# First projections by halves of the features, and rotary scores over 128 rows, in a two-layer hybrid decoder trunk

## The chip, the cores and the metric

The kernel runs on one core of a Trainium2 chip. The metric is the time of one execution on the device in microseconds (us), lower is better. TensorE is called PE in the profile, VectorE DVE, ScalarE ACT, GpSimd POOL and SyncE SP; PEld is TensorE's weight load, which goes beside its matmuls.

## The reference

Two layers on 512 tokens of 1024 features, f32. Each layer is a half-step SwiGLU, a mixer of three branches, and a second half-step SwiGLU, each with a LayerNorm behind it.

```python
def swiglu(x, w_gate, w_up, w_down):               # 1024 -> 2816 -> 1024
    return (jax.nn.silu(x @ w_gate) * (x @ w_up)) @ w_down
...
def causal_block_attention(q_nope, q_rope, k_nope, k_rope, v):   # 4 heads, 128 + 64 features
    ...
        s = (jnp.einsum('bqhd,bkhd->bhqk', q_nope[:, q0:q1], k_nope[:, :q1])
             + jnp.einsum('bqhr,bkr->bhqk', q_rope[:, q0:q1], k_rope[:, :q1])).astype(jnp.float32) * scale
...
    for l in range(DEPTH):
        h = layer_norm(DEEPNORM_ALPHA * h + 0.5 * swiglu(h, ...), ln1_g[l], ln1_b[l])
        mix = hybrid_mixer(h, cos, sin, ...)
        h = layer_norm(DEEPNORM_ALPHA * h + mix, ln2_g[l], ln2_b[l])
        h = layer_norm(DEEPNORM_ALPHA * h + 0.5 * swiglu(h, ...), ln3_g[l], ln3_b[l])
```

The mixer projects x by one combined matrix. Its branches are a gated DeltaNet (short convolutions of 4 taps on q, k and v, a delta rule in chunks of 64, an output norm), a convolution of 31 taps over 512 channels, and a latent attention with 4 heads, whose score has a part of 128 features per head and a rotary part of 64, for which all heads share one key. Three sigmoid gates weight them.

## The kernel before

**Numbers.** Each f32 product with a weight is taken as three matmuls of a rounded f32 form (`mm3`): ACT casts the high part, DVE subtracts it to get the low part, for x (`xh`, `xl`) and for every weight (`s` tiles from a `raw` buffer). The scores and the delta rule's small products go in plain f32, each of which the trace shows as two instructions.

**Order.** All instructions are recorded by a planner class and issued afterwards, so nearly every row of the profile names one line, L287. The planner keeps a cost for each instruction (`_cost`), a priority (the clock of PE at which it was recorded, plus a bias that `pl.stream` sets), and the number of free buffers, and lists instructions for each engine by simulating them. A changed cost or bias can therefore move instructions anywhere in the program. Engines run their lists in order. All DMAs are issued from SP.

**Start.** x comes in 8 pieces `s<-in_x` of 128 tokens by 512 features. `to_features` transposes each on PE with an identity (`ident`), casts it to `xh` on ACT, subtracts on DVE to `xl`, and copies the f32 form to `xf` on ACT. Each FFN begins with `proj_first`: four banks (gate and up for the first two blocks of 128 hidden columns), each by half of the tokens (256 columns) over all 8 feature blocks of 128. The first weights are loaded as whole blocks of 512 KB. After these, pairs of blocks go through `seven`, a Strassen-like scheme of seven products, for which `block_sums` prepares differences of x blocks on DVE (8 subtractions and 16 halves of splits per FFN).

**Mixer.** `proj_first` gives the rotary key, the decay and beta logits and two of the keys. A chain of small gate instructions on DVE and ACT leads to the chunk factors; keys are scaled on ACT (`s<-s,rky`) and transposed on PE. `short_conv` makes q, k and v from a bank by one ACT copy and three DVE steps, then a tanh. The 31-tap convolution goes on DVE as filler work all through the mixer, 4 blocks of 30 steps, whose results are transposed on PE. The attention keeps a rotary query `qr` for a pair of heads in 128 rows, 64 per head, and the shared rotary key twice, in rows 0 to 63 and 64 to 127 of `krope`; the rotary score of a head uses its 64 rows of both.

```python
PE.matmul(ps[:, 0:n], lhsT=qn[h][:, c], rhs=kn[h][:, 0:n], start=True, stop=False)
PE.matmul(ps[:, 0:n], lhsT=qr[h // 2][hr, c], rhs=krope[hr, 0:n], start=False, stop=True)
```

Row block i of 4 has n = 128 (i + 1) columns. The scores go to a mask, a maximum, an exponential and PE transposes of the probabilities.

## Time and profile before

| | |
|---|---|
| median of three runs | 2466.42 us |
| the runs | 2465.38, 2466.42, 3408.69 us |
| profiled execution | 2464.4 us, its span 2462.6 us |
| granted TensorE clock, mean | 0.998 |
| busy: PE, PEld, DVE, ACT | 2438.4, 2207.6, 2044.8, 1267.1 us |
| chain that ended last | 95% PE, 2% DVE, 2% ACT |

The span is the time from the first to the last instruction in the profile; the execution's own time lies 1.8 us above it. The busy time of an engine is the time in which it worked at something, at whatever pace. The chain is followed back from the last instruction, each time to what released it or to the one before on its engine. Rows of a timeline merge neighbouring instructions of one form; the bracket tells how long the engine was idle before the row and what ended that.

### The profile page before, as it was taken

The numbers are of one execution on the slowest core, as the hardware profiler recorded it, in microseconds if no ns is written. First come the engines' busy times: TensorE is split into PE (matmuls) and PEld (weight loads), VectorE is DVE, ScalarE is ACT, GpSimd is POOL, SyncE is SP. The second block draws the span as 40 slices with busy tenths as digits, with TensorE's granted clock in tenths as the row PEclk, the third lists the DMA queues.
The fourth block names the chain that finished last, engine by engine and source line by source line (L and its number), as shares of the span: only waits on it lengthen the run. The fifth ranks groups of instructions, "written<-read, shape, count | busy, mean of one in ns | idle before, by whom it ended". The sixth has DMA issues, their size and how long they took to land.

```text
span 2462.6 us, 41114 instructions
## 1 busy us (share of the span) xinstructions
PE 2438.4 (99%) x15860; PEld 2207.6 (90%) x15860; DVE 2044.8 (83%) x4197; ACT 1267.1 (51%) x2781; POOL 0.2 (0%) x4
## 2 busy tenths in 40 slices
PE   8999999999999999999999999999999999999998
PEld 8999887888799899998899998878878998999986
DVE  7998467999999799984699883689999987999844
ACT  6655328436646446553356552383366464565530
POOL 0000000000000000000000000000000000000000
PEclk9999999999999999999999999999999999999999
DMA  5434452312233623344333353513122335233431
GB/s 164 115 109 142 131 145 82 94 53 72 83 98 102 190 78 108 107 125 141 120 95 104 110 172 101 155 51 103 34 81 86 104 103 180 86 104 105 146 121 49
DMA packets 268804, 267.71 MB, mean 109 GB/s; under 512 B 17652, under 2 KB 220608, under 8 KB 268608
## 3 DMA queue, kind: packets, MB, share of 16 engines
q1 hardware_dynamic: 268608, 265.08, 36.0%
q8 instruction: 124, 2.03, 0.3%
q14 instruction: 72, 0.59, 0.1%
HBM read 247.74 MB, written 17.30 MB: 108 GB/s over the span
## 4 chain that ended last, share of the span: by engine, by line
PE 95%; DVE 2%; ACT 2%; issue 0%; DMA 0%; SPq 0%; DVEq 0%; ACTq 0%
PE ps L287 95%; DVE s L287 2%; ACT s L287 1%; ACT ps L287 0%; ACT xh L287 0%; DMA s<-in_x 0%; DVE xl L287 0%; DVE lnt L287 0%; DVE lny L287 0%; SPq L287 0%; DVE st L287 0%; DVEq L1293 0%; DVE mv L287 0%; DVE lnv L287 0%; DVE neg_eg L287 0%
## 5 line engine op out<-in xcount | busy, mean ns | idle before, releaser
L287 PE MATMUL ps<-s 128*128 128x256 f32 (+3 forms) x9212 | 1561.3, 324 | 0.0
L287 PEld LDWEIGHTS ps<-s 128*128 128x128 f32 (+1 forms) x9212 | 1351.2, 190 | 154.8 <-issue 17.0
L287 PE MATMUL ps<-xh,s 128*128 128x256 f32 (+2 forms) x4064 | 900.2, 308 | 2.8 <-ACT s L287 1.8
L287 PEld LDWEIGHTS ps<-xh,s 128*128 128x128 f32 (+1 forms) x4064 | 678.2, 191 | 36.5 <-ACT s L287 2.2
L287 DVE TENSOR_TENSOR s<-raw,s 128x512 fp32r<-128x512 f32 (+1 forms) x844 | 548.8, 681 | 138.0 <-PE ps L287 53.3
L287 PE MATMUL ps<-xl,s 128*128 128x256 f32 (+2 forms) x2032 | 623.6, 307 | 0.1
L287 DVE TENSOR_TENSOR s<-s 128x512 fp32r<-128x512 f32 (+10 forms) x1014 | 591.3, 612 | 29.1 <-ACT s L287 13.7
L287 ACT CAST s<-raw 128x512 fp32r<-128x512 f32 (+1 forms) x740 | 433.9, 619 | 225.4 <-PE ps L287 162.1
L287 ACT CAST s<-s 128x512 fp32r<-128x512 f32 (+1 forms) x642 | 358.4, 593 | 221.4 <-DVE s L287 189.9
L287 ACT COPY s<-ps 128x256 f32<-128x256 f32 (+3 forms) x664 | 257.4, 400 | 379.8 <-PE ps L287 378.0
L287 PEld LDWEIGHTS ps<-xl,s 128*128 128x128 f32 (+1 forms) x2032 | 387.2, 191 | 17.6 <-DVE xl L287 0.5
L287 DVE SCALAR_TENSOR_TENSOR s<-s 128x512 f32<-128x512 f32 (+26 forms) x356 | 249.7, 712 | 1.4 <-ACT s L287 1.1
L287 DVE TENSOR_TENSOR s<-ps,s 128x256 f32<-128x256 f32 (+1 forms) x336 | 147.5, 439 | 87.9 <-PE ps L287 74.7
L287 ACT ACTIVATE s<-s 128x512 f32<-128x512 f32 x162 | 103.3, 667 | 84.6 <-DVE s L287 83.5
L287 DVE SCALAR_TENSOR_TENSOR s<-s,ps 128x512 f32<-128x512 f32 x96 | 64.6, 680 | 91.5 <-PE ps L287 89.9
L287 DVE TENSOR_TENSOR s<-raw 128x512 f32<-128x512 f32 x208 | 139.6, 683 | 0.0
L287 PE MATMUL ps<-ident,s 128*128 128x128 f32 (+1 forms) x508 | 86.5, 284 | 12.1 <-DVE s L287 4.7
L287 PEld LDWEIGHTS ps<-ident,s 128*128 128x128 f32 (+1 forms) x508 | 61.3, 143 | 36.2 <-issue 12.7
L287 ACT CAST xh<-ps 128x512 fp32r<-128x512 f32 x48 | 28.6, 595 | 126.5 <-PE ps L287 126.4
L287 DVE TENSOR_TENSOR s<-s,raw 128x512 f32<-128x512 f32 x104 | 71.0, 683 | 0.1
L287 DVE SCALAR_TENSOR_TENSOR s<-ps,s 128x510 f32<-128x510 f32 (+3 forms) x88 | 63.1, 739 | 2.1 <-PE ps L287 1.7
L287 ACT ACTIVATE s<-ps,s 128x512 f32<-128x512 f32 x58 | 40.3, 718 | 45.0 <-PE ps L287 44.6
(100 smaller groups left out, 552.0 us busy)
## 6 DMA issues: line engine op xcount, KB each, us to landing
raw<-in_w_in SPq DMA_DIRECT2D x106, 512.0 KB, 3.9
raw<-in_ffn_w_gate SPq DMA_DIRECT2D x88, 512.0 KB, 3.7
raw<-in_ffn_w_up SPq DMA_DIRECT2D x88, 512.0 KB, 3.8
raw<-in_ffn_w_down SPq DMA_DIRECT2D x88, 512.0 KB, 4.9
spill<-s SPq DMA_DIRECT2D x40, 256.0 KB, 2.0
s<-spill SPq DMA_DIRECT2D x40, 256.0 KB, 2.6
raw<-in_w_out SPq DMA_DIRECT2D x16, 512.0 KB, 4.3
s<-in_x SPq DMA_DIRECT2D x16, 256.0 KB, 3.8
```

What stands on the lines that cost most here:

```text
L287: self.issued = o["f"](*o["a"], **o["k"])
```

## The change

The FFNs' four first weights are loaded in two halves of 256 KB by features (`wblock_first`), the second half with a later bias; `proj_first` (in the FFNs and the mixer) goes for each token half through the first four feature blocks of all its banks, then through the last four. At the very start, x's first two token blocks are loaded by feature halves: both first halves, the four weights' first halves, both second halves, the weights' second halves. The bias of `block_sums` goes from 4 to 6, and the copies to `xf` get 3 more. The planner's costs are corrected: 90 ns for DVE on less than 128 partitions, ACT by the number of operands, DMAs at 330 instead of 200 bytes per ns. The rotary scores use all 128 rows: `krope` gets zeros in rows 64 to 127 (a memset on POOL), and a second tile `kr2` zeros in rows 0 to 63 (POOL) and the copied key in rows 64 to 127 (DVE), so that the other head's queries are multiplied by zeros.

```diff
@@ -122,16 +122,17 @@
             fast = name in ("tensor_scalar", "tensor_copy") and not psum
             if name in ("bn_stats", "bn_aggr", "reduce_max"):
                 n = max(n, ins[0].free_size())
-            return 70 + 57 * min(vectors, 1) + n * (0.52 if fast else 1.04)
+            part = 90 if o.shape[0] < 128 else 0
+            return 70 + part + 57 * min(vectors, 1) + n * (0.52 if fast else 1.04)
         if engine == "ACT":
             c = (52 if psum else 94) + 0.83 * max(n, 64)
             if o.shape[0] < 128 and o.shape[0] % 32 == 0:
                 c += 110
-            c += 93 * sum(hasattr(k.get(x), "tensor") for x in ("scale", "bias", "accum_out"))
+            c += 93 * (len(ins) - 1) + 126 * (len(outs) - 1)
             return c
         if engine == "POOL":
             return 125 + n * {"tensor_tensor": 2.15, "tensor_scalar": 0.9}.get(name, 1.0)
-        return max(500.0, n * o.shape[0] * 4 / 200.0)
+        return max(500.0, n * o.shape[0] * 4 / DMA_RATE)
 
     def _record(self, engine, name, fn, a, k):
         isap = lambda x: hasattr(x, "tensor")
@@ -288,14 +289,16 @@
 
 
 LOCK = True
-X_BIAS = 2.5
-XF_BIAS = 4.0
+DMA_RATE = 330.0
+X_BIAS = 3.9
+XF_BIAS = 4.6
 FIRST_BIAS = 0.1
-SUM_BIAS = 4.0
+SECOND_BIAS = 0.6
+SUM_BIAS = 6.0
 TAIL = 6
 TAIL_OUT = 4
 WINDOW = 150.0
-KEEP_LATER = 0.0
+KEEP_LATER = 3.0
 SILU_BIAS = 30.0
 PARAMS_AHEAD = 15.0
 RAWS = 5
@@ -402,10 +405,11 @@
             S.copy(h, src)
             (eng or V).tensor_tensor(lo, src, h.bitcast(F32), op=SUB)
 
-        def weight(shape, pieces, hold=False):
+        def weight(shape, pieces, hold=False, biases=None):
             raw = pl.tile(wraw_p, shape, F32, "raw", RAWS)
-            for sl, src in pieces:
-                Q.dma_start(out=raw[sl], in_=src)
+            for i, (sl, src) in enumerate(pieces):
+                with pl.stream(bias=pl.bias + biases[i] if biases else None):
+                    Q.dma_start(out=raw[sl], in_=src)
             n = shape[1]
             step = n if raw.free_size() <= 512 else n // 2
             hs, ls = [], []
@@ -427,6 +431,12 @@
             s = block(src)
             return weight(list(s.shape), [(ALL, s)], hold)
 
+        def wblock_first(src, i):
+
+            s = block(src)
+            halves = [(slice(None), slice(k, k + 4)) for k in (0, 4)]
+            return weight(list(s.shape), [(sl, s[sl]) for sl in halves], True, [FIRST_BIAS * i, SECOND_BIAS + FIRST_BIAS * i])
+
         def split(src):
             h, lo = slot(F32R), slot(F32R)
             split_into(h, lo, src)
@@ -437,15 +447,16 @@
             PE.matmul(ps, lhsT=lh, rhs=rl, start=False, stop=False, skip_group_check=more)
             PE.matmul(ps, lhsT=ll, rhs=rh, start=False, stop=stop, skip_group_check=more)
 
-        def proj(ps, w, c0=0, c1=T):
-            for k in range(KD):
+        def proj(ps, w, c0=0, c1=T, ks=range(KD)):
+            for k in ks:
                 mm3(ps[:, c0:c1], w[0][k], w[1][k], xh[:, k, c0:c1], xl[:, k, c0:c1],
                     k == 0, k == KD - 1)
 
         def proj_first(items):
             for c0 in (0, 256):
-                for ps, w in items:
-                    proj(ps, w, c0, c0 + 256)
+                for k0 in (0, 4):
+                    for ps, w in items:
+                        proj(ps, w, c0, c0 + 256, range(k0, k0 + 4))
 
         def transposes(ps, blocks):
             for j, b in enumerate(blocks):
@@ -472,8 +483,8 @@
 
         xf = {}
 
-        def to_features(tt, store):
-            for g in range(2):
+        def to_features(tt, store, groups=(0, 1)):
+            for g in groups:
                 ps = bank()
                 transposes(ps, quarters(res.pop((tt, g))))
                 c = slice(tt * 128, (tt + 1) * 128)
@@ -653,8 +664,7 @@
             first = []
             for f in range(PLAIN):
                 for w in (wg, wu):
-                    with pl.stream(bias=FIRST_BIAS * len(first)):
-                        first.append((bank(), wblock(cols(w, f), True)))
+                    first.append((bank(), wblock_first(cols(w, f), len(first))))
 
             tx = None
             with pl.stream(bias=SUM_BIAS):
@@ -1080,6 +1090,12 @@
                 S.copy(kr[64 * g:64 * g + 64], kr_sb[0:64])
             krope = rope(kr, swapped(kr_sb, (0, 0)))
 
+            kr2 = slot()
+            G.memset(kr2[0:64], 0.0)
+            V.tensor_copy(kr2[64:128], krope[64:128])
+            G.memset(krope[64:128], 0.0)
+            kropes = krope, kr2
+
 
             og = []
             for h in range(H):
@@ -1149,14 +1165,13 @@
 
             ao = []
             for h in range(H):
-                hr = slice(64 * (h % 2), 64 * (h % 2) + 64)
                 pt = [slot() for _ in range(4)]
                 for i in range(NT):
                     n = (i + 1) * 128
                     c = slice(i * 128, n)
                     ps = bank()
                     PE.matmul(ps[:, 0:n], lhsT=qn[h][:, c], rhs=kn[h][:, 0:n], start=True, stop=False)
-                    PE.matmul(ps[:, 0:n], lhsT=qr[h // 2][hr, c], rhs=krope[hr, 0:n], start=False, stop=True)
+                    PE.matmul(ps[:, 0:n], lhsT=qr[h // 2][:, c], rhs=kropes[h % 2][:, 0:n], start=False, stop=True)
                     V.tensor_tensor(ps[:, c], ps[:, c], C("amask"), op=ADD)
                     mx = small([128, 1], "mx")
                     V.reduce_max(mx, ps[:, 0:n], axis=mybir.AxisListType.X)
@@ -1267,9 +1282,13 @@
         for tt in range(NT):
             for hf in range(2):
                 res[tt, hf] = slot()
-                with pl.stream(bias=X_BIAS if tt > 1 else 0):
+                with pl.stream(bias=(X_BIAS if hf else 0) if tt < 2 else XF_BIAS):
                     Q.dma_start(out=res[tt, hf], in_=a["x"][0, tt * 128:(tt + 1) * 128, hf * 512:(hf + 1) * 512])
-            with pl.stream(bias=XF_BIAS if tt > 1 else 0):
+        for g in range(2):
+            for tt in range(2):
+                to_features(tt, False, [g])
+        for tt in range(2, NT):
+            with pl.stream(bias=XF_BIAS):
                 to_features(tt, False)
         for l in range(DEPTH):
             ffn(l, a["ffn1_w_gate"], a["ffn1_w_up"], a["ffn1_w_down"], a["ln1_g"], a["ln1_b"],
```

**Start, the queue on SP.** In the loads, s_81 to s_88 are pieces of x and raw_106, raw_112, raw_118 and raw_124 the four first weights. Before:

```order
L287 DMA s_81<-in_x 128x512
L287 DMA s_82<-in_x 128x512
L287 DMA s_87<-in_x 128x512
L287 DMA s_88<-in_x 128x512
L287 DMA raw_106<-in_ffn1_w_gate 128x8x128
L287 DMA raw_112<-in_ffn1_w_up 128x8x128
L287 DMA raw_118<-in_ffn1_w_gate 128x8x128
L287 DMA raw_124<-in_ffn1_w_up 128x8x128
```

And now:

```order
L288 DMA s_81<-in_x 128x512
L288 DMA s_83<-in_x 128x512
L288 DMA raw_106<-in_ffn1_w_gate 128x4x128
L288 DMA raw_112<-in_ffn1_w_up 128x4x128
L288 DMA raw_118<-in_ffn1_w_gate 128x4x128
L288 DMA raw_124<-in_ffn1_w_up 128x4x128
L288 DMA s_82<-in_x 128x512
L288 DMA s_84<-in_x 128x512
L288 DMA raw_106<-in_ffn1_w_gate 128x4x128
L288 DMA raw_112<-in_ffn1_w_up 128x4x128
```

One x piece (token block 1, first features) and four half weights stand directly behind the first x piece; the other feature halves of x come behind the four half weights.

**Mixer, DVE, layer 1.** ps_1020 is the bank of the q projection of the first head, s_1021 its short convolution, s_1022 the activated q, ps_1030 and s_1031 the same for the second head; s_999 to s_1014 and s_994 are the chunk work (keys by keys with the decay). Before:

```order
L287 SCALAR_TENSOR_TENSOR s_1014<-ps_1013,beta_944,s_1011 128x128
L287 SCALAR_TENSOR_TENSOR s_1021<-ps_1020,s_915,s_1021 128x511
L287 TENSOR_TENSOR s_994<-s_1014,s_912 32x128
L287 SCALAR_TENSOR_TENSOR s_1021<-ps_1020,s_915,s_1021 128x510
L287 TENSOR_TENSOR s_994<-s_1014,s_912 32x128
L287 SCALAR_TENSOR_TENSOR s_1021<-ps_1020,s_915,s_1021 128x509
L287 TENSOR_TENSOR s_994<-s_1014,s_912 32x128
L287 SCALAR_TENSOR_TENSOR s_1031<-ps_1030,s_915,s_1031 128x511
L287 TENSOR_TENSOR s_994<-s_1014,s_912 32x128
L287 SCALAR_TENSOR_TENSOR s_1031<-ps_1030,s_915,s_1031 128x510
L287 SCALAR_TENSOR_TENSOR s_1022<-s_1022,s_1021 128x512
```

And now:

```order
L288 SCALAR_TENSOR_TENSOR s_1021<-ps_1020,s_915,s_1021 128x509
L288 SCALAR_TENSOR_TENSOR rky_984<-rkt_985,rky_984 128x16
L288 SCALAR_TENSOR_TENSOR s_1031<-ps_1030,s_915,s_1031 128x511
L288 TENSOR_TENSOR s_1081<-raw_1079,s_1080 128x512
L288 SCALAR_TENSOR_TENSOR s_1022<-s_1022,s_1021 128x512
L288 SCALAR_TENSOR_TENSOR s_1031<-ps_1030,s_915,s_1031 128x510
L288 TENSOR_TENSOR s_1083<-raw_1079,s_1082 128x512
L288 SCALAR_TENSOR_TENSOR s_1031<-ps_1030,s_915,s_1031 128x509
L288 TENSOR_TENSOR s_1086<-raw_1084,s_1085 128x512
L288 SCALAR_TENSOR_TENSOR s_999<-ps_998,beta_944,s_996 128x128 x4
L288 TENSOR_TENSOR s_994<-s_999,s_912 32x128 x2
```

The last step of the first q convolution and its activation (s_1022) stood at the end of the chunk work, and now stand ahead of it, among the small steps of the gate chain (rky_984) and the weight splits.

**Attention, PE, layer 1.** Behind `<-` stand the moving and the stationary tile: ps_1434 to ps_1449 (now ps_1435 to ps_1450) are the first head's four score banks, ps_1461 (ps_1462) the second's; s_1330 is `krope`, s_1332 the new `kr2`, s_1376 (s_1377) the rotary queries of the first pair of heads. Before:

```order
L287 MATMUL ps_1434<-s_1408,s_1406 128x128
L287 MATMUL ps_1434<-s_1330,s_1376 128x128
L287 MATMUL ps_1439<-s_1408,s_1406 128x256
L287 MATMUL ps_1439<-s_1330,s_1376 128x256
L287 MATMUL ps_1444<-s_1408,s_1406 128x384
L287 MATMUL ps_1444<-s_1330,s_1376 128x384
L287 MATMUL ps_1449<-s_1408,s_1406 128x512
L287 MATMUL ps_1449<-s_1330,s_1376 128x512
L287 MATMUL ps_1438<-ident_75,s_1436 128x128
L287 MATMUL ps_1461<-s_1415,s_1413 128x128
L287 MATMUL ps_1461<-s_1330,s_1376 128x128
```

And now:

```order
L288 MATMUL ps_1435<-s_1409,s_1407 128x128
L288 MATMUL ps_1435<-s_1330,s_1377 128x128
L288 MATMUL ps_1440<-s_1409,s_1407 128x256
L288 MATMUL ps_1440<-s_1330,s_1377 128x256
L288 MATMUL ps_1445<-s_1409,s_1407 128x384
L288 MATMUL ps_1445<-s_1330,s_1377 128x384
L288 MATMUL ps_1450<-s_1409,s_1407 128x512
L288 MATMUL ps_1450<-s_1330,s_1377 128x512
L288 MATMUL ps_1439<-ident_75,s_1437 128x128
L288 MATMUL ps_1462<-s_1416,s_1414 128x128
L288 MATMUL ps_1462<-s_1332,s_1377 128x128
```

The places are the same; the second head's rotary part takes the tile with the key in the upper rows, and both rotary parts now run over 128 rows (which the names alone show by s_1332 in place of s_1330).

## Rows read from the trace of the kernel before

**Rows 1.** The page: span, busy time of the engines, and shares of the chain that ended last by engine.

```profile
span 2462.6 us, 41114 instructions
...
PE 2438.4 (99%) x15860; PEld 2207.6 (90%) x15860; DVE 2044.8 (83%) x4197; ACT 1267.1 (51%) x2781; POOL 0.2 (0%) x4
...
PE 95%; DVE 2%; ACT 2%; issue 0%; DMA 0%; SPq 0%; DVEq 0%; ACTq 0%
```

**Rows 2.** The waits of PE over the whole run: who waited for whom, us in total, times, longest.

```profile
PE ps L287 <- DVE s L287: 4.7, 5, 2.1
...
PE ps L287 <- DMA s<-in_x: 4.6, 2, 4.3
...
PE ps L287 <- ACT s L287: 4.3, 3, 1.8
```

**Rows 3.** The timeline of the start, PE and ACT (start us, duration us, engine, line, operation, out<-in, count, and in brackets the idle time before with what ended it).

```profile
4.32 1.94 PE L287 MATMUL ps<-ident,s 128*128 128x128 f32 x8 [4.32 <-DMA s<-in_x]
...
6.55 1.97 PE L287 MATMUL ps<-ident,s 128*128 128x128 f32 x8 [0.29 <-DMA s<-in_x]
...
10.32 0.58 PE L287 MATMUL ps<-xh,s 128*128 128x256 f32 x1 [1.81 <-ACT s L287]
...
11.13 0.79 PE L287 MATMUL ps<-xh,s 128*128 128x256 f32 x2
...
9.65 1.14 ACT L287 CAST s<-raw 128x512 fp32r<-128x512 f32 x2
...
11.46 1.14 ACT L287 CAST s<-raw 128x512 fp32r<-128x512 f32 x2 [0.67 <-DMA raw<-in_ffn_w_up]
```

**Rows 4.** Windows of the start: us, then busy time and count of PE, PEld, DVE, ACT and POOL, the granted clock of PE (1.00 is full speed), DMA share, GB/s.

```profile
11.13:13.90 2.77, 2.77 (x13) 2.77 (x14) 1.84 (x3) 1.77 (x4) 0.00 (x0) 1.00 1.18 300
...
13.90:20.00 6.10, 6.10 (x52) 6.10 (x52) 2.59 (x4) 1.65 (x3) 0.00 (x0) 1.00 1.07 360
```

**Rows 5.** The timeline of PE at the end of one head pair's scores and at the products of the softmax with v, and the 64-row matmuls over the whole run, the widest and the narrowest of four forms (512, 384, 256 and 128 columns, x16 each; busy us, mean ns).

```profile
615.48 0.91 PE L287 MATMUL ps<-s 64*128 64x384 f32 x2
...
616.32 1.13 PE L287 MATMUL ps<-s 128*128 128x512 f32 x2
...
617.38 1.12 PE L287 MATMUL ps<-s 64*128 64x512 f32 x2
...
644.16 1.06 PE L287 MATMUL ps<-s 128*128 128x512 f32 x2
...
645.06 0.81 PE L287 MATMUL ps<-s 128*128 128x384 f32 x2
...
645.71 0.59 PE L287 MATMUL ps<-s 128*128 128x256 f32 x2
...
L287 PE MATMUL ps<-s 64*128 64x512 f32 x16 | 9.0, 641 | 0.0
...
L287 PE MATMUL ps<-s 64*128 64x128 f32 x16 | 3.9, 322 | 0.0
```

**Rows 6.** The timeline of the mixer's start in layer 1: PE, ACT and DVE.

```profile
395.26 0.47 PE L287 MATMUL ps<-xh,s 128*128 128x512 f32 x1 [0.47 <-ACT ps L287]
...
408.36 1.86 ACT L287 ACTIVATE s<-s,rky 128x128 f32<-128x128 f32 x6
...
408.82 0.91 PE L287 MATMUL ps<-ident,s 128*128 128x128 f32 x3 [1.25 <-ACT s L287]
...
413.00 0.61 DVE L287 SCALAR_TENSOR_TENSOR s<-ps,beta,s 128x128 f32<-128x128 f32 x2 [4.83 <-PE ps L287]
...
427.70 0.63 PE L287 MATMUL ps<-ident,s 128*128 128x128 f32 x4 [2.04 <-DVE s L287]
...
428.16 0.61 PE L287 MATMUL ps<-s 128*128 128x128 f32 x4
```

**Rows 7.** The timeline at the transposes of the delta rule's output: ACT and PE.

```profile
597.17 4.79 ACT L287 ACTIVATE s<-s,rky 128x128 f32<-128x128 f32 x16
...
596.42 1.53 PE L287 MATMUL ps<-s 128*128 128x512 f32 x6
...
597.78 0.46 PE L287 MATMUL ps<-ident,s 128*128 128x128 f32 x2
...
602.10 0.48 PE L287 MATMUL ps<-s 128*128 128x512 f32 x1
```

**Rows 8.** Windows (columns as in rows 4): DVE in the first FFN, at the mixer's start, and behind it; and layer 2 where the granted clock falls.

```profile
26.00:40.00 14.00, 14.00 (x117) 14.00 (x118) 14.00 (x31) 10.38 (x26) 0.00 (x0) 1.00 0.01 2
...
400.00:430.00 30.00, 26.71 (x143) 21.53 (x143) 22.74 (x67) 29.27 (x93) 0.00 (x0) 1.00 0.20 53
...
480.00:530.00 50.00, 50.00 (x230) 41.34 (x229) 50.00 (x118) 19.60 (x34) 0.00 (x0) 1.00 0.23 61
...
700.00:750.00 50.00, 50.00 (x356) 47.04 (x356) 50.00 (x101) 24.77 (x49) 0.00 (x0) 1.00 0.33 96
...
1632.00:1636.00 4.00, 4.00 (x21) 3.81 (x21) 0.53 (x3) 3.19 (x10) 0.00 (x0) 0.57 0.01 4
```

**Rows 9.** The timeline of DVE in the first FFN.

```profile
26.98 7.85 DVE L287 TENSOR_TENSOR s<-s 128x512 f32<-128x512 f32 x20
```

**Rows 10.** The chain that ended last (start us, us, engine, tile, count), its end.

```profile
2113.77 339.64 PE ps L287 x2359
...
2453.43 0.70 DVE s L287
```

## The prediction

> **What bounds the kernel now.** I read the busy line and the chain of the page first: TensorE (PE) is busy for 2438.4 us of a span of 2462.6, and 95% of the chain that ends last is PE [rows 1]. So the time falls only where PE waits, where a PE instruction takes longer than its like, or at the two ends. Next I read the waits of PE: 4.7 us on VectorE (DVE), 4.6 us on the loads of x, 4.3 us on ScalarE (ACT) [rows 2]. A busy PE need not be at its pace, so I then looked at the starts of single instructions. That gave three more things that the busy line hides: matmuls at half pace after the start, transposes that follow ACT's pace, and extra time wherever a 64-row matmul stands beside 128-row ones. Last I read how full DVE is behind PE, since PE can only gain what DVE can deliver [rows 8].
>
> **The start.** Before, PE begins at 4.32 us when x's first piece is there, and its first projection at 10.32 us, after 1.81 us of waiting for ACT to cast the first weight, which ACT starts at 9.65 [rows 3]. Weights come one per 1.81 us (casts at 9.65 and 11.46 [rows 3]), 512 KB each, so I estimate 0.9 us for a half. In the new order only x's two first pieces stand ahead of the weights. The third piece of before was used at 6.55 [rows 3], two places behind the first, so I put x's second piece at 5.4, then weight halves at 6.3, 7.2, 8.1 and 9.0, the other x pieces at 9.9 and 10.8, the second halves from 11.7 on. ACT is the server there: the x casts and copies take 0.6 each, the first weight half's cast 0.57 (two in 1.14 [rows 3]). They give a first matmul near 7.6 and an unbroken row of them from about 8.7, where before it is unbroken from 11.13. That is 2.4 us earlier. But eight transposes that before ran inside that wait (for x's other halves) now stand between matmuls: 0.115 us each at full pace (four in 0.46 us [rows 6]), 0.21 at the pace of the start; I take 1.2 us. Net **-1.2**, from 0 to -2. The 48 matmuls of the first feature half last at least 48 x 0.117 = 5.6 us, to 14.3, and the second weight halves have until then: 11.7 + 1.3 for cast and subtraction.
>
> PE's pace in the first 2.8 us of projections is 13 matmuls in 2.77 us, 0.213 each, afterwards 52 in 6.10 us, 0.117 each, while the granted clock reads 1.00 in both [rows 4]. I keep the length of the slow stretch as it is. If pieces of 256 KB do not come in proportion but at 1.1 us, as x's two did between 4.32 and 6.55 [rows 3], the first weight is 0.2 us later and the last second half 1.6, which the 14.3 still covers. The Trainium skill ("DMA: Bandwidth & Descriptors", section Bandwidth) speaks against the halves: its rule is to batch DMAs to 1 MiB or more for three quarters of the peak rate. By it the sum would be some 0.2 higher, by the 1.1 us of the row just named, and by proportion as it stands.
>
> **The rotary scores.** Each score bank gets qn x kn over 128 rows, then the rotary part over 64 rows; each of these f32 matmuls shows as two instructions. 64 of the 64-row instructions stand in the program, 16 for each of four widths [rows 5], that is 32 pairs and 64 changes of form. With 384 columns, a pair of 64 rows begins at 615.48 and the next at 616.32, 0.84 apart; 128-row pairs undisturbed are 0.65 apart (645.06 to 645.71). With 512 columns it is 1.06 (616.32 to 617.38) against 0.90 (644.16 to 645.06) [rows 5]. So a change of form costs 0.19 by the one width and 0.16 by the other. The form alone costs it: inside a pair the second instruction follows at the same pace with either. 64 x 0.19 = **-12.1** after taking 0.04 off for the eight changes that lead into transposes; 64 x 0.16 = -10.2 is the other end. What is added: per layer two memsets on POOL and a copy of 64x512 on DVE. No such memset is in the trace; its nearest rows are the small ones of the start. I bound it at 0 and 1.5 us of POOL, long before the first score, and nobody waits: 0.
>
> The Trainium skill ("TensorEngine Tiling (Array Packing)", section When to Use Tiling) speaks the other way: with a contraction of 64 or less, row tiling may give up to twice the rate, and 128 rows with half zeros waste that. Nothing is forfeited by row here, since 64-row pairs already run one after the other at the 128-row pace. The same page (Key Properties) says that a change of tiling mode drains TensorE, which agrees with the 0.19.
>
> **The waits at the mixer's start.** In each layer PE waits 0.47 us (395.26), 1.25 us (408.82) and 2.04 us (427.70) [rows 6]. Around 408.82 transposes of scaled keys go at ACT's pace: six ACT instructions in 1.86 us, 0.31 each, against 0.115. With such transposes to 415, I count 7.0 us per layer over the pace that the same instructions have elsewhere (4.1 idle, 1.2 in restarts, 1.7 in pacing). DVE meanwhile waits 4.83 us for PE until 413.00 [rows 6], and the short convolutions that end the 2.04 us wait come only behind the work of that moment. The new order puts the q convolution into this idle time, so its transposes can run before the chunk work. DVE's small dependent steps go on beside it. From the order and these durations I find some 3.5 us of waits left per layer (1.3 for the gate transposes, 0.9 for the keys, 0.4 for q, the rest pacing), so **-3.5** per layer, -7.0 in all; ends 0 and -9.
>
> **The output transposes.** After the delta rule 16 transposes and six 512-column matmuls take 597.78 to 602.10, 4.32 us, behind 16 ACT instructions in 4.79 us. At the pace of the rows around (six matmuls from 596.42 to 597.78, 0.227 each, transposes 0.115) it would be 16 x 0.115 + 6 x 0.227 = 3.2 [rows 7]. The new order spreads them between matmuls. Of the 1.1 us I take 1.0 per layer, **-2.0**; ends 0 and -2.2.
>
> **What DVE gives back.** DVE is 100% busy at 480 to 530 and 700 to 750, but not at 400 to 430 (22.74 of 30 us) [rows 8]. PE does not wait for it there, but if PE comes earlier by 8 to 10 us per layer, the convolution taps that fill DVE come due against it. In the order, the last taps' transposes stand at nearly the same place of PE's work as before, while DVE has 3 to 6 us more ahead of them; DVE's idle time at the mixer's start, now used, pays most of it. I take **+2.5** per layer, +5; ends 0 and +6 per layer.
>
> **Block sums.** Ahead of its Strassen products each FFN takes 8 differences of x blocks and 16 split halves on DVE; in the first FFN 20 of these 24 stand in one row of 7.85 us from 26.98, while DVE is 100% busy from 26 to 40 [rows 8, 9]. The new bias asks for them later, but in the order they stay ahead of the first gate product in the first FFN as before, with only two weight splits and a weight sum coming right behind. I take 0, ends -0.5 and +2 over the four FFNs. The tail behind the last matmul (last chain rows [rows 10]) holds the same instructions in the same order: 0.
>
> The sum on the profiled time of 2464.4 us (span 2462.6): 2464.4 - 1.2 - 12.1 - 7.0 - 2.0 + 5.0 = 2447.1. The median of the three runs, 2466.4, lies 2 us above it, so I forecast **2449**.
>
> **The rivals.** First, DVE is the bound (chance 0.15): from 430 to 750 us it is almost full, so a rotary saving of 6 us per layer turns into a wait for the last convolution taps. Then of each layer only what DVE wins ahead of that stretch remains, some 3 of the 7 us that it idles in 400 to 430: 2466.4 - 1.2 - 2 x 3 = about 2459. For it: 100% in two windows; against it: the same idle time, which is as large as the layer's gain [rows 8]. It shows as PE waits on DVE between 700 and 750.
> Second, the mixer's order brings nothing (0.17): the waits of 1.25 and 2.04 move but stay as long, since ACT's 0.31 per transposed block is unchanged. Then 2466.4 - 1.2 - 12.1 = about 2453, with less given back by DVE.
> Third, the clock (0.07): PE waits a few us at the start and at the mixer; in layer 2 the granted clock fell to 0.57 from 1632 to 1636, just behind such a wait [rows 8]. At 1.00 the same work would take 4 x 0.43 = 1.7 us less. If the new waits make it fall in both layers and the start's slow pace lasts twice as long (13 x 0.096 = 1.25), the time is 2449 + 3 = 2452. The Trainium skill ("TensorE: Matmul & The Clock Gate", section Part 1) calls the throttled state the default, which activity releases. The slow pace at the start agrees, the granted clock of 1.00 beside it does not [rows 4].
> Fourth, **slower than before** (0.03): block sums that come later in an FFN whose DVE has no slack (100% busy, 26 to 40). If PE waits for them in all four FFNs, it decides from 17 / 4 = 4.3 us per FFN on; at the whole row of 7.85 us for 20, so 9.4 for 24 [rows 9], it gives 2449 + 38 = 2487.
> That it does not do what it says (0.03): the load order could be met by the queue in another way, and then only the rotary part remains, 2454.
>
> **How the numbers follow.** The forecast has 0.55. The terms' ends, added as independent, are about +-6 us. The range reaches up over the DVE rival, and down to where the mixer gives its full 9 us and DVE takes nothing: 2440 to 2460. A measurement of this kernel can tell about 2%, 49 us, from no change: faster by that would need 2417, which no row offers (0.01); slower by that needs 17 us more in each FFN (0.01); within 0.98.
>
> **What would show it.** Right: no PE instruction of 64 rows; scores of a 384-column pair 0.65 apart; first projection near 7.6 us; the q convolution's transposes ahead of the chunk work with a wait under 0.6 us. DVE's waits would be at most some 2 us longer between 600 and 740. Wrong: PE waits on DVE around 717 to 737 of several us; waits of PE inside an FFN; or 128-row rotary pairs that still start 0.84 apart.

## The result and the profile after

The changed kernel takes 2442.2 us in the median of four runs (2441.48 to 2443.37), against 2466.42 for the kernel before (2465.38 to 2467.89): a ratio of 0.9902 with an interval of 0.9882 to 0.9921. One of the four runs of the kernel before, at 3408.69 us, was in a slower state and is left out of both. The difference, 24 us, lies under the 2% that the prediction took as the smallest change to be told, but the interval stays well below 1, and the sign is the forecast one; 2442.2 is inside the range of 2440 to 2460, near its lower end, and 7 us under the forecast of 2449. Between the two profiled executions it is 2464.4 to 2442.45, 21.9 us in the span.

The page of the kernel after, its first line, busy times and chain (the lines of [rows 1]):

```profile
span 2440.7 us, 41173 instructions
...
PE 2421.4 (99%) x15860; PEld 2207.6 (90%) x15860; DVE 2043.0 (84%) x4199; ACT 1271.4 (52%) x2781; POOL 2.3 (0%) x8
...
PE 91%; DVE 5%; ACT 3%; DMA 1%; issue 1%; SPq 0%; DVEq 0%; ACTq 0%
```

PE is busy for 17 us less with as many instructions, so most of the gain is in instructions that follow one another sooner. The waits of PE after, the answer to [rows 2]:

```profile
PE ps L288 <- DMA s<-in_x: 4.5, 2, 4.2
PE ps L288 <- ACT s L288: 3.5, 5, 1.2
PE ps L288 <- DVE s L288: 1.2, 4, 0.6
PE ps L288 <- DVE gpl L288: 0.5, 2, 0.2
```

The waits on DVE have gone from 4.7 us to 1.7, the longest from 2.1 to 0.6.

To see where the 21.9 us came from, I took for each PE instruction the time from the end of the one before it to its own end, and subtracted the median that this pair of forms has in the trace (a form is rows, columns and width, plain f32 apart from the rounded form). What is over the median is time lost to waiting, pacing or the clock; the sum of the medians is the pure work, and it holds the price of a change of form. It is an estimate, and other ways to group the forms move the difference in pure work by up to 1 us. Stage by stage, both layers:

| | before | after | difference |
|---|---|---|---|
| pure work of PE (the sum of medians) | 2421.6 | 2409.5 | -12.1 |
| up to the first matmul's end, and the first 30 us of work | 11.2 | 9.4 | -1.8 |
| mixer's start, layer 1 and layer 2 | 6.7, 7.7 | 2.4, 2.3 | -9.7 |
| stretch with the transposes of the delta rule's output | 1.44, 1.43 | 1.09, 0.91 | -0.9 |
| attention, convolution taps, branches and the start of the second FFN | 0.75, 0.76 | 1.03, 1.06 | +0.6 |
| the four FFNs behind their start, to the next stage | 0.71, 0.56, 0.76, -0.12 | 1.51, 0.92, 1.00, 0.25 | +1.8 |
| tail behind the last matmul | 9.19 | 9.24 | +0.05 |

The differences sum to -22 with rounding; a negative loss is scatter about the medians. The first FFN's 1.51 holds a wait of 0.58 us for DVE, 0.80 over the median, at the first transposes of x behind it:

```profile
360.12 0.65 PE L288 MATMUL ps<-ident,s 128*128 128x128 f32 x4 [0.58 <-DVE s L288]
```

The same place before, at 368.83 us, is 0.43 over the median and is counted with the FFN too.

**The rotary scores** (timeline of PE, two 512-column products and two rotary instructions of one head, then transposes):

```profile
614.68 1.88 PE L288 MATMUL ps<-s 128*128 128x512 f32 x4
...
616.40 0.60 PE L288 MATMUL ps<-ident,s 128*128 128x128 f32 x4
```

The four start within 616.40 - 614.68 = 1.72 us, 0.43 each, product and rotary part alike. Before, the same four took from 616.32 [rows 5] to the transpose behind them at 618.43:

```profile
618.43 0.33 PE L287 MATMUL ps<-ident,s 128*128 128x128 f32 x1
```

That is 2.11 us, with a change of form on either side of the rotary part.

**The start** (timeline of PE and ACT, the answer to [rows 3]):

```profile
4.16 1.09 PE L288 MATMUL ps<-ident,s 128*128 128x128 f32 x4 [4.16 <-DMA s<-in_x]
...
7.90 0.58 PE L288 MATMUL ps<-xh,s 128*128 128x256 f32 x1 [1.19 <-ACT s L288]
...
7.23 1.79 ACT L288 CAST s<-raw 128x512 fp32r<-128x512 f32 x3
```

The first projection starts at 7.90 where 7.6 was forecast, and runs on without a gap from 8.49 (8.7 was forecast). The slow pace is there as in [rows 4]: 13 matmuls in the 2.51 us from 8.49 to 11.00, 53 in the 6.00 us from 13.00 to 19.00, each count with those cut by an edge. Instruction by instruction it is 0.213 us up to about 12.3 and 0.12 behind that; before, the pace rises at 14.07. The windows print a granted clock of 1.00 for all of this, which is no reading (see the last section).

**The mixer's start**, layer 1 (timeline of PE, the answer to [rows 6]):

```profile
392.10 0.63 PE L288 MATMUL ps<-ident,s 128*128 128x128 f32 x4 [0.23 <-DVE gpl L288]
...
410.52 0.33 PE L288 MATMUL ps<-ident,s 128*128 128x128 f32 x1 [0.54 <-ACT s L288]
...
411.52 0.71 PE L288 MATMUL ps<-ident,s 128*128 128x128 f32 x5
...
431.91 0.66 PE L288 MATMUL ps<-ident,s 128*128 128x128 f32 x4 [0.23 <-DVE s L288]
```

The 1.25 us ahead of the keys' transposes have become 0.54, and these go between matmuls instead of one after another at ACT's pace. Those of the first q convolution are among the row at 411.52, which runs on to 412.17 behind the end of the window, without a wait. The 2.04 us ahead of 427.70 are gone; the transposes at 431.91, of a later head, wait 0.23.

**DVE and the clock** (windows; the first kernel is the one before, in a stretch that [rows 8] does not show):

```profile
600.00:650.00 50.00, 50.00 (x210) 31.05 (x210) 45.53 (x125) 35.42 (x109) 0.00 (x0) 1.00 0.26 74
```

```profile
584.00:634.00 50.00, 49.30 (x226) 36.25 (x225) 49.47 (x138) 41.20 (x117) 0.52 (x1) 1.00 0.29 90
...
1620.00:1650.00 30.00, 29.23 (x176) 24.66 (x175) 29.07 (x69) 29.32 (x91) 0.00 (x0) 1.00 0.28 71
```

Among the scores DVE had 4.5 us of idle time before, and has 0.5 after. The second row of after is the mixer's start of layer 2, at a granted clock of 1.00 throughout, where [rows 8] has a stretch at 0.57.

### The profile page after: what moved, and what is told of

It reads as the page before. It is cut to its first block, busy times and chain, and to the rows that moved or that the text cites. A ratio compares the mean times of both kernels' runs of the same rounds, so it can differ in the third digit from the quotient of the medians.

```text
span 2440.7 us, 41173 instructions
## 1 busy us (share of the span) xinstructions
PE 2421.4 (99%) x15860; PEld 2207.6 (90%) x15860; DVE 2043.0 (84%) x4199; ACT 1271.4 (52%) x2781; POOL 2.3 (0%) x8
## 4 chain that ended last, share of the span: by engine, by line
PE 91%; DVE 5%; ACT 3%; DMA 1%; issue 1%; SPq 0%; DVEq 0%; ACTq 0%
PE ps L288 91%; DVE s L288 4%; ACT s L288 2%; DMA raw<-in_mla_w_o 1%; ACT ps L288 0%; DMA raw<-in_w_in 0%; DMA s<-in_x 0%; ACT xh L288 0%; DVE xl L288 0%; SPq L288 0%; DVE lnt L288 0%; DVE lny L288 0%; DVE rkt L288 0%; ACT L288 0%; DVE rky L288 0%
## 5 line engine op out<-in xcount | busy, mean ns | idle before, releaser
L288 PEld LDWEIGHTS ps<-s 128*128 128x128 f32 x9212 | 1351.1, 190 | 144.8 <-issue 5.8
L288 ACT COPY s<-ps 128x256 f32<-128x256 f32 (+4 forms) x664 | 258.3, 400 | 369.3 <-PE ps L288 366.9
L288 PEld LDWEIGHTS ps<-xl,s 128*128 128x128 f32 (+1 forms) x2032 | 386.9, 190 | 16.8 <-DVE xl L288 0.2
```

The source lines that it names most:

```text
L288: self.issued = o["f"](*o["a"], **o["k"])
```

## The experiments

The changed kernel was timed with the result alone, the kernel before anew beside each group of experiments, with medians from 2465.58 to 2466.42 us. So times above or below the changed kernel are good to about 1 us.

### The rotary scores alone, and all but them

The first kernel is the one before with the new rotary scores only:

```diff
-PE.matmul(ps[:, 0:n], lhsT=qr[h // 2][hr, c], rhs=krope[hr, 0:n], start=False, stop=True)
+PE.matmul(ps[:, 0:n], lhsT=qr[h // 2][:, c], rhs=kropes[h % 2][:, 0:n], start=False, stop=True)
```

> The kernel before with the 128-row rotary scores alone (second key tile, memsets, copy), nothing else of the change. Theory (a change of form costs 0.19 us, 64 of them, and DVE has room for it in its idle time among the scores, 600 to 650 us of the kernel before): the time falls by 12.1 us to about 2454, no 64-row matmul is left, and PE waits no longer on DVE than in the kernel before. Rival (DVE is the bound from 430 to 750 us): the time falls by 0 to 6 us and PE waits on DVE for 3 to 6 us per layer ahead of the last convolution blocks.

Measured: 2452.65 us against 2465.8 for the kernel before, ratio 0.9948 (0.9933 to 0.9963): 13.1 us less in the medians, 12.2 in the spans of the two profiles. No 64-row matmul is left, and PE has no wait at all between 586 and 745 us, as before. The window that answers to the one above:

```profile
600.00:650.00 50.00, 50.00 (x238) 36.59 (x238) 49.12 (x133) 41.10 (x128) 0.00 (x0) 1.00 0.26 75
```

DVE went from 45.53 to 49.12 of 50 us: the idle time took what PE's earlier arrival asked for. That DVE is the bound is refuted here.

The second is the changed kernel with the line of before put back, and the second key tile out.

> The changed kernel with the 64-row rotary scores of before. Theory: 12.1 us more than the changed kernel, about 2454, all of it between the first and the last score of each layer (6.05 us each), and the short waits at the mixer's start stay as in the changed kernel. Rival (the saving came with the new order, not with the form): within 4 us of the changed kernel.

Measured: 2454.15 us, 12.0 above the changed kernel; the span 11.7 above; PE's waits on ACT, DVE and the gate chain are 2.9, 1.2 and 0.5 us, where the changed kernel has 3.5, 1.2 and 0.5. The saving belongs to the form, and it adds to the rest without a loss that these numbers could show.

### More work for DVE in the attention

Eight instructions of 128x512 per layer, in both kernels:

```diff
+                    if i % 2 == 0:
+                        V.scalar_tensor_tensor(extra, kn[0], 0.5, kn[0], op0=MUL, op1=ADD)
```

> The kernel before with eight more DVE instructions of 128x512 in each layer's attention (their result goes nowhere), 5.3 us per layer. Theory (DVE was idle for 4.5 us between 600 and 650 us, so it has this much to give): the time rises by at most 2 us in all. Rival (DVE is the bound there): it rises by 8 to 11 us, with PE waits on DVE between 600 and 745 us.

Measured: 2465.82 us against 2465.58, ratio 1.0001 (0.9992 to 1.0011). The time does not move, but not for the reason given. Its windows, and below them the later one of the kernel before:

```profile
600.00:650.00 50.00, 50.00 (x212) 31.07 (x212) 45.39 (x124) 35.28 (x107) 0.00 (x0) 1.00 0.23 74
...
750.00:800.00 50.00, 50.00 (x354) 46.84 (x353) 48.52 (x100) 33.80 (x64) 0.00 (x0) 1.00 0.33 97
```

```profile
750.00:800.00 50.00, 50.00 (x355) 46.91 (x354) 44.82 (x78) 34.82 (x67) 0.00 (x0) 1.00 0.35 102
```

DVE is still idle for 4.6 us among the scores; the added work has pushed other work back into 750 to 800, where 3.7 us more are busy. The first block of convolution results is transposed at 728.6 instead of 717.8, the last at 752.8 instead of 737.6: the planner, which knows of the added work, gives PE other matmuls in their place.

> The changed kernel with the same eight DVE instructions per layer, 5.3 us. Theory (the change has used up DVE's idle time among the scores, 0.5 us of 50 are left): PE now waits on DVE, the time rises by 6 to 11 us. Rival (PE's reserve ahead of the last convolution blocks is larger than DVE's idle time says): it rises by less than 3 us.

Measured: 2443.83 us, 1.6 above the changed kernel for 10.6 us of added DVE work (2.2 by the ratios to the kernel before), and no wait of PE on any engine from 560 to 760 us in layer 1. The rival holds. Here too the last transposes move, from 733.0 to 744.2.

### The start

x and the first weights loaded whole, and first projections over all features at once:

```diff
-                for k0 in (0, 4):
-                    for ps, w in items:
-                        proj(ps, w, c0, c0 + 256, range(k0, k0 + 4))
+                for ps, w in items:
+                    proj(ps, w, c0, c0 + 256)
...
-                    first.append((bank(), wblock_first(cols(w, f), len(first))))
+                    with pl.stream(bias=FIRST_BIAS * len(first)):
+                        first.append((bank(), wblock(cols(w, f), True)))
```

> The changed kernel with x and the first weights loaded whole and in the order of before, and all first projections over all eight feature blocks at once; costs, block sums and rotary scores as in the changed kernel. Theory (the start alone gains by the halves): first projection back at 10.3 us instead of 7.9, time 1.5 to 2 us above the changed kernel, the waits at the mixer's start unchanged at some 3 us per layer. Rival (the halves in the mixer's first projections are what shortens the waits there): 7 to 10 us above, with waits of 6 to 7 us per layer at the mixer's start.

Measured: 2447.61 us, 5.4 above the changed kernel, between the two expectations. In the span it is 4.7, and by the reckoning of the table above 1.4 of these are at the start, 0.9 in the first FFN, 1.0 at the two mixers' starts (3.0 and 2.8 us), the rest in pieces of 0.1 to 0.7 over the mixers. So the halves with their load order are worth 1.4 us at the start, and the mixer's start hardly depends on them. The rest is what another list does; why it is worse was not settled.

> The changed kernel with the two biases of before for the block sums and the copies of x (4 and 0 instead of 6 and 3). Theory (later sums cost the FFNs 0.2 to 0.4 us each in small waits of PE): the time falls by about 1 us, and PE's small waits inside the four FFNs go back from 2.6 to 1.5 us. Rival: no difference in them, or the start gets longer by 1 us or more since the sums then stand among the first casts.

```diff
-KEEP_LATER = 3.0
+KEEP_LATER = 0.0
...
-SUM_BIAS = 6.0
+SUM_BIAS = 4.0
```

Measured: 2448.46 us, 6.3 above the changed kernel: against the theory, and as the rival's second half said. The timeline of DVE and PE in the first FFN, of this kernel:

```profile
20.99 9.66 DVE L288 TENSOR_TENSOR s<-s 128x512 f32<-128x512 f32 x23
...
30.56 0.69 DVE L288 TENSOR_TENSOR xl<-ps,xh 128x512 fp32r<-128x512 f32 x1
...
31.40 0.53 PE L288 MATMUL ps<-xh,s 128*128 128x256 f32 x1 [4.58 <-DVE xl L288]
```

With the old biases 23 instructions for the block sums stand in front of the subtraction that gives the low part of x's last token block, and PE waits 4.58 us for that. Behind the wait the granted clock falls: its mean from 31.4 to 35.0 us is 0.53. By the reckoning of the table the start loses 16.8 us here, against 9.4 in the changed kernel and 11.2 before. In the FFNs the earlier sums save 0.9 us in all. So the later sums cost the FFNs little waits, but in this new order they, or the later copies, are what keeps the start from losing more than it gains. (The two biases were not taken apart.)

### The planner's costs

> The changed kernel with the planner's costs of before (DVE on part of the partitions, ACT operands, DMA rate). Theory (the corrected costs make the planner start the short convolutions in DVE's idle time, and this is the gain at the mixer's start): the time is 7 to 9 us above the changed kernel, with waits and pacing of 6 to 7 us per layer between 375 and 432 us. Rival (the gain there comes from the halves of the first projections or the other biases): within 2 us of the changed kernel.

```diff
-DMA_RATE = 330.0
+DMA_RATE = 200.0
...
-            part = 90 if o.shape[0] < 128 else 0
+            part = 0
...
-            c += 93 * (len(ins) - 1) + 126 * (len(outs) - 1)
+            c += 93 * sum(hasattr(k.get(x), "tensor") for x in ("scale", "bias", "accum_out"))
```

Measured: 2455.16 us, 13.0 above the changed kernel, more than either expectation. The losses at the mixer's start are 8.2 and 6.7 us, with waits of 1.2 us for the keys and 2.05 for the q convolution, nearly those of [rows 6]; the start of the program loses 3.8 us more than the changed kernel's, which the theory had not counted. So the costs account for all of the gain at the mixer's start, and the order of the start needs them as well. One thing more is in the windows of this kernel:

```profile
430.00:434.00 4.00, 4.00 (x17) 3.54 (x16) 4.00 (x8) 2.56 (x11) 0.00 (x0) 0.57 0.00 0
```

The fall of the clock, which before stood in layer 2, is here in layer 1, behind the 2.05 us wait.

> The changed kernel with one number undone: the planner's DMA rate of 200 instead of 330. Theory (the planner believes that the weights of the first q and k projections land late, records them late, and this alone decides where the q convolution stands on DVE): the q convolution is behind the chunk work again, the waits and the pacing at the mixer's start are 6 to 8 us per layer as before, the time is 10 to 13 us above the changed kernel. Rival (the costs of DVE and ACT do it): within 3 us of the changed kernel.

```diff
-DMA_RATE = 330.0
+DMA_RATE = 200.0
```

Measured: 2447.35 us, 5.2 above the changed kernel, between the two expectations. The losses at the mixer's start are 3.3 us in each layer instead of 6 to 8, though the q convolution is behind the chunk work again. The theory falls: the DMA rate does move q, but where q stands on DVE is not what decides the waits. In this kernel the keys' transposes stand apart between matmuls as in the changed one, the wait ahead of them is 0.85 us, and the one for q 0.64. Most of the 5.2 us lies elsewhere: the start of the program loses 13.2 us, 3.8 more than the changed kernel's and as much as with all the old costs, and the first projection comes at 9.21 us instead of 7.90. The four FFNs, on the other hand, lose 1.9 us less than in the changed kernel, as little as in the kernel before.

> The kernel before with that one number changed, a DMA rate of 330. Theory (the DMA rate decides the mixer's start, and the other parts add little there): waits and pacing there fall from 7 to 3 to 5 us per layer, the time falls by 5 to 9 us. Rival: within 3 us of the kernel before, since without the other costs the end of the q convolution stays behind the chunk work.

```diff
-        return max(500.0, n * o.shape[0] * 4 / 200.0)
+        return max(500.0, n * o.shape[0] * 4 / 330.0)
```

Measured: 2463.92 us against 2466.08, ratio 0.9992 (0.9982 to 1.0001); the losses at the mixer's start are 5.6 and 5.5 us. The time is the rival's (2.2 us less), and its reason holds in part: the steps of the first q convolution now run ahead of the chunk work (from 409.92, the chunk work from 418.26 us), but its activation stays behind it at 427.13, and PE waits 1.17 us for that. What the mixer's start gains, the start of the program and the FFNs mostly lose again (1.6 and 2.3 us more than in the kernel before).

Put together, for the mixer's start in the two layers: in the changed kernel 8.2 and 6.7 us with the old costs, 3.3 and 3.3 with the new costs of DVE and ACT alone, 2.4 and 2.3 with the DMA rate too; in the kernel before 6.7 and 7.7 with the old costs, 5.6 and 5.5 with the new DMA rate alone. The larger part is that of DVE and ACT. It fits that the planner now gives a scaled ACT copy with its scale column its real length and puts a matmul between two transposes that wait for it, but the costs of ACT and DVE were not taken apart, so this is argued and not shown.

### Rows of the array

> The changed kernel with four rows of eight extra f32 matmuls of 512 columns in layer 1 ahead of the attention (results go nowhere), each row alternating between two banks: 64 rows of the same half; 64 rows of the lower and the upper half in turn; 128 rows; 64 and 128 rows in turn. Theory (each change of form costs 0.19 us, and a matmul with 64 rows takes as long as one with 128): 0.86 us each for the first and third row, 1.05 each for the fourth. For the second row: 0.86 if the halves follow one another, 0.43 if two halves run at once, 1.05 if a change of half costs as much as a change of form.

```diff
+            if l == 0:
+                lo, hi, full = slice(0, 64), slice(64, 128), slice(0, 128)
+                for forms in ((lo, lo), (lo, hi), (full, full), (lo, full)):
+                    ba, bb = bank(), bank()
+                    for _ in range(4):
+                        for b, r in zip((ba, bb), forms):
+                            PE.matmul(b, lhsT=kn[0][r, 0:128], rhs=qn[0][r], start=True, stop=True)
```

One profiled run. Windows of PE over the four rows of matmuls (us, busy time and instructions of PE, PEclk, DMA share, GB/s; each matmul shows as two instructions, those cut by an edge count in both windows, and the last of the first row run beside the first of the second):

```profile
607.37:613.49 6.12, 6.12 (x15) 1.00 0.14 34
...
613.49:617.87 4.38, 4.38 (x19) 1.00 0.30 83
...
617.87:624.93 7.06, 7.06 (x17) 1.00 0.46 142
...
624.93:633.27 8.34, 8.34 (x17) 1.00 0.00 0
```

Instruction by instruction, the first and the third row go at 0.429 us each, 0.86 for a matmul, and the fourth at 0.52 to 0.53, 1.05 for a matmul: a change of form costs 0.195 us each way, with nothing else near. The second row was the surprise. Lower and upper halves in turn take 0.43 us for a matmul: they run two at a time. Their instructions start in two series, each 0.43 us apart: at 614.46, 614.89, 615.32 and 615.75 us, and between them at 614.35, 614.78, 615.21 and 615.64.

So a better version keeps 64 rows, and gives both halves something to do (GROUPS is ((0, 1), (2, 3))):

```diff
+                for group in GROUPS:
+                    for i in group:
+                        for g in range(2):
+                            ps = banks[i, g] = bank()
+                            PE.matmul(ps[:, 0:n], lhsT=qn[h0 + g][:, i * 128:n], rhs=kn[h0 + g][:, 0:n], start=True, stop=False)
+                    for i in group:
+                        for g in range(2):
+                            hr = slice(64 * g, 64 * g + 64)
+                            PE.matmul(banks[i, g][:, 0:n], lhsT=qr[h0 // 2][hr, i * 128:n], rhs=krope[hr, 0:n], start=False, stop=True)
```

(The planner is told to issue the rotary matmuls of a group one behind the other, and that each costs half as much by its columns.)

> The changed kernel with 64-row rotary scores again, but for two heads in turn, one in the lower and one in the upper rows of the array: for two row blocks at a time the four qn x kn products, then the four rotary ones without anything in between. Theory (two halves run at once, as the extra matmuls showed with 0.43 us for a pair of 512-column matmuls in each half; one change of form to and fro for four of them): per pair of heads 4.3 us of rotary matmuls become 2.15 and 2 x 2 x 0.195 = 0.8 us of changes, so 1.35 us less, four times in the program: 5.4 us less than the changed kernel, about 2437. Rival (the scores come in bunches, and the masks and exponentials behind them make PE wait): within 3 us of the changed kernel or above it, with PE waits on DVE or ACT among the scores.

Measured: 2439.68 us (2439.26 to 2440.75) against 2466.08 for the kernel before, ratio 0.9892 (0.9878 to 0.9907). Its timeline of PE, and its waits:

```profile
612.73 1.77 PE L295 MATMUL ps<-s 64*128 64x384 f32 x8
```

```profile
PE ps L295 <- ACT s L295: 3.8, 7, 1.2
...
PE ps L295 <- DVE mx L295: 0.7, 2, 0.3
```

Eight rotary instructions, four of 384 columns and four of 512, take 1.70 us up to the next start (614.44); at 0.32 and 0.43 each they would be 3.0. Over the whole trace the eight groups take 10.2 us and the changes around them 1.4 more, where the changed kernel's 64 rotary instructions take 17.2: the form itself gives 5.6 us, as forecast. But the median is only 2.5 us under the changed kernel; their ranges do not touch. Of the 2.9 us that are missing, 0.7 are a new wait on DVE's maxima and 0.3 more wait on ACT; the rest was not traced to its place.

> The same with row blocks in three groups (first; second and third; fourth) instead of two pairs, so that fewer scores come at once. Theory: one change of form to and fro more per pair of heads, 4 x 0.39 = 1.6 us above the kernel with two groups by the matmuls, about 2438.5, less whatever that one waits among its scores. Rival: the waits among the scores are the larger part, and this one is 1 us or more below the kernel with two groups.

```diff
-GROUPS = ((0, 1), (2, 3))
+GROUPS = ((0,), (1, 2), (3,))
```

Measured: 2439.54 us (2438.59 to 2440.82), ratio 0.9891 (0.9877 to 0.9906): the same as with two groups, neither 1.6 above nor 1 below. PE has no wait on DVE's maxima here. What the further change of form costs and what the waits had cost come out even, which both expectations allow; this pair doesn't tell them apart. Either is the best kernel of the study.

## Why the prediction was right, and where its steps were off

- **Rotary scores: -12.1, measured -12.1** in the pure work, -12.2 in the span when done alone, +11.7 when undone. The agreement to a tenth is luck, the size is not. The 0.19 us per change was right from one width, and 0.195 is what the extra matmuls show; the 0.16 from the other width came of a pair taken as undisturbed at 0.90 us, where 0.86 is the undisturbed one. The sentence that nothing is forfeited by the row was wrong: two 64-row matmuls in different halves run at once. The trace of before could not show it, since there the two instructions of a rotary matmul lie in one half and a 128-row product stands between two of them. The Trainium skill ("TensorEngine Tiling (Array Packing)", section Theoretical Speedup) says up to twice the rate for a small dimension of 64 or less; 0.43 against 0.86 us agrees with it, and 2.5 us of it were gained here.
- **The start: -1.2, measured -1.8.** First projection at 7.90 (7.6), unbroken from 8.49 (8.7). The gain needs more than the halves that the sum named: with the old DMA rate the new start loses 2.0 us more than the old one did, with the old biases for sums and copies 5.6 more.
- **The mixer's start: -7.0, measured -9.7.** The waits left are 2.4 us per layer, where I had 3.5. The rest of the difference is in layer 2, which gains 5.4 where layer 1 gains 4.3: in the changed kernel's profile the fall of the clock at 1632 is gone. I had priced that fall at 4 x 0.43 = 1.7 us in the rival, and left it out of the sum; the kernel with the new rotary scores alone, whose waits are the old ones and whose clock does not fall there, loses 1.0 us less in layer 2 than the kernel before. That the mixer's order brings nothing, the second rival, is refuted: the waits do not stay as long, 1.25 became 0.54 and 2.04 went. That q moves into DVE's idle time was the reason given; with the old DMA rate q stands late again and most of the gain stays, so that reason was not the main one.
- **The output transposes: -2.0, measured -0.9** for the stretch. They do go between matmuls, but the first one still waits 0.70 us for ACT, which was not in the sum:

```profile
591.79 0.33 PE L288 MATMUL ps<-ident,s 128*128 128x128 f32 x1 [0.70 <-ACT s L288]
```

- **What DVE gives back: +5.0, measured +0.6.** This is the step that was mis-sized most; PE waits for DVE nowhere between 560 and 760 us in layer 1. I set DVE's work against the place of the taps' transposes in a fixed list, with 100% windows on both sides of the one that mattered: between 600 and 650 DVE was idle for 4.5 us. And the list is not fixed: with 5.3 us more of DVE work per layer the planner moves these transposes by 10 to 15 us and gives PE other matmuls meanwhile. The DVE rival falls with it.
- **Block sums: 0, measured +1.8** in the four FFNs, as small waits (the largest inside an FFN 0.41 us over the median, at 44.11). Not all of it is theirs: with the old biases the FFNs lose 0.9 us less, but with the old DMA rate and the sums still late 1.9 less, and the new rate in the kernel before adds 2.3. So it comes mostly with the DMA rate, which the sum had at nothing there. The rival mechanism, sums in the way of PE, is real, but on the other side: it appears when the change to the bias is undone (4.58 us).
- **The clock rival** went the other way: fewer waits, and no fall at either mixer's start of the changed kernel's profile. Its remark that a granted clock of 1.00 stands beside the slow start was a misreading: the trace has no record of the clock there (last section).

Over all, 4.4 us too much for DVE, 2.7 too little at the mixer's start and 0.6 at the program's, against 1.1 too much at the output transposes and 1.8 missing in the FFNs, make -17.3 into about -22. The other 2 us between 2449 and 2442.2 are those that I added for the median: the kernel before has runs of 2465.4 to 2467.9 beside a profiled one of 2464.4, the changed one a median 0.25 below its profiled run.

## What to carry to other kernels

A matmul over half of the rows between full ones costs two changes of form, here 0.195 us each, however short it is: either fill it up with zeros to the full rows, or group several of them, and then alternate the halves of the array so that two run at once (0.43 us against 0.86 for a matmul). When a later engine looks full, read its idle time in the window that holds the work in question, and ask whether its consumers can move; a list made by a planner lets them. Costs of a planner are worth measuring against the trace: undoing them cost 13 us here, the DMA rate alone 5, most of that at the start of the program, and the two biases for sums and copies 6.

## What was not expected of the hardware

- f32 matmuls over rows 0 to 63 and rows 64 to 127, issued in turn, take 0.43 us per matmul of 512 columns against 0.86 when all lie in one half.
- The granted clock fell behind a wait at the mixer's start in one layer of three profiles: a mean of 0.57 from 1632 to 1636 in the kernel before and 0.60 in the one with more DVE work, there behind the wait for the keys (1.25 us up to 1629.93 in the kernel before), and 0.57 from 430 to 434 with the old costs, behind the 2.05 us wait. It fell in no profile in both layers, and with the new rotary scores alone in neither, though the waits there are as long (1.23 us at 1624.59, 2.06 at 1643.46). So such a wait is a risk to the clock, not a certainty; the changed kernel's longest wait there is 0.58 us, and its clock stays at 1.00. In the kernel with the old biases it fell in the first FFN, behind the 4.58 us wait.
- The first projections run at about half pace, 0.213 us for an instruction of 256 columns against 0.12 later, and the windows print a granted clock of 1.00 beside it. But the trace's first record of the clock, at full, begins at 14.07 us in the kernel before and at 12.26 in the changed one, just where the pace rises; a window without a record prints 1.00. Two profiles of the study have an earlier record, and their means from 12 to 16 us are 0.60 and 0.67. This is the one with the new rotary scores alone:

```profile
12.00:16.00 4.00, 4.00 (x24) 4.00 (x23) 2.67 (x6) 2.87 (x6) 0.00 (x0) 0.60 1.07 331
```

Its record is at half (1.2 of 2.4 GHz) from 11.76 to 15.17 us, and the matmuls there go at 0.213 us, at 0.12 behind it. So the start runs at the lower of the two levels, as far as the same pace shows it where no record lies.
